# Gate and up product by token instead of by feature, in a one-layer trunk kernel

## The chip, the cores and the metric

The kernel runs on one core of a Trainium2 chip (trn2). The metric is device time in microseconds from launch to end, in several executions; the kernel before has a median of 1082.83 us in 3 runs (1080.88 to 1083.24). PE is the tensor engine, PEld its loading of the operand that stands still, DVE the vector engine, ACT the scalar engine, POOL the GpSimd engine, SP the queue that starts the weight loads.

## The reference

One layer over 256 tokens of width 2048, all in float32. Cut to the part that matters here:

```python
def rmsnorm(x, g):
    return x * lax.rsqrt(jnp.mean(x * x, axis=-1, keepdims=True) + RMS_EPS) * g

x = x + jnp.einsum('bsm,md->bsd', y, w_out)          # y: the two head groups, normalised
h2 = rmsnorm(x, norm2_g)
act = jax.nn.silu(jnp.einsum('bsd,df->bsf', h2, w_gate)) * jnp.einsum('bsd,df->bsf', h2, w_up)
x = x + jnp.einsum('bsf,fd->bsd', act, w_down)       # w_gate, w_up: [2048, 5632]; w_down: [5632, 2048]
```

Ahead of it stands a projection of x to five sections of 1024 columns (v, C, h_B, u, B) with a spatial gating and a short convolution; behind it a last RMSNorm.

## The kernel before

**Precision.** Every matrix operand is cut into a high and a low part of the type float32r (`split`: ACT casts the high part at L82, DVE subtracts it from the source at L83). A product is three products: high by high, low by high, high by low.

**Two forms of product.** The token-major form (`mm_tok`, L121 to L123) holds 128 features of 128 tokens still and moves 512 weight columns, three matmuls of 512 columns. The feature-major form (`mm_feat`, L129 and L130) holds 128 x 128 weights still and moves activations: first the high and the low part of all 256 tokens side by side (512 columns), then with the low weights the high part alone (256 columns). Its result is a PSUM bank of two halves that have to be added (`sum_halves`: ACT copies one half at L152, DVE adds the other at L154).

**Stages.** In order: v (token-major), C with h_B, u, B, w_out (all feature-major, names `ch`, `u`, `b`, `o`), gate and up (feature-major, `gu`), w_down (token-major, `d`). Before the change `gu` runs over 44 tiles f of 128 hidden features, a gate tile and an up tile at once.

**Weights.** They come as units of [128, 2048], each in two halves of 512 KB: one load on SP into `raw` (5 buffers), one cast on ACT to `whi` and one subtraction on DVE to `wlo` (4 buffers each). `next_unit` asks for the next unit when one is taken, so a half is cast into the buffer that the half four places ahead of it has just left. A unit of `gu` feeds 16 matmul pairs.

**Behind each tile f** (`act`, L446 to L453): the two halves are added, the gate is multiplied by 1/rms of its token (`r2b`, a row that every partition holds), ACT takes its sigmoid, DVE multiplies twice, and the result is cut into `aT`, which w_down reads by contraction tile. 1/rms itself needs the sum of squares `sq1`, which POOL gathers behind the last pair of w_out; PE adds it up over the partitions with four small matmuls (`ps_n`, L180), and spreads it over the partitions with one more (`ps_n2b`, L194). The up product keeps its 1/rms open until w_down's result.

**Beside it** `residual` (L456 to L461) turns x to token-major in 8 groups of four 128 x 128 transposes on PE (`ps_x`), for w_down's end.

The order on each engine is made by the tile framework's scheduler from the order of the code and from its own estimates; an engine does its instructions in that order, and waits where an operand or a buffer isn't there.

Of the kernel before, what the change touches and what calls it, by code (L numbers as in the profile page):

```python
# [10 lines left out]
F32 = mybir.dt.float32  # L11
# [5 lines left out]
P = 128  # L17
NW = 512          # one PSUM bank of float32
UN = 2048         # a weight unit is [P, UN], one contiguous load
# [11 lines left out]
def trunk_layer_kernel(  # L31
# [4 lines left out]
    """xt: per-feature vectors as columns, then x by feature, [P, KD, T]; wsj [j, h, i].  # L36

    weights: units of v, (C, h), u, B, out, (gate, up), down in the order of use.
    A token-major product keeps the activations still and moves 512 weight columns;
    a feature-major one keeps 128 weight columns still and moves the high and the low  # L40
    part of all tokens side by side, which leaves the two halves of a bank to be added.
    """
    nc = tc.nc
    T, D = out.shape                  # 256, 2048
    KD = D // P                       # 16
    AW = ln_g.shape[1]                # 1024
    H = wsj.shape[1]                  # 8
    NT = T // P                       # 2 token tiles = gMLP blocks
    KA = AW // P                      # 8
    NC = D // NW                      # 4  # L50
    CA = AW // NW                     # 2
    w_v, w_ch, w_u, w_b, w_o, w_gu, w_d = weights
    NF = w_gu.shape[0] // 2           # 44 tiles of the hidden layer
    KU = UN // NW                     # 4 contraction tiles of a token-major unit

# [34 lines left out]
    def load_unit(piece=HU, between=None):  # L90
        """two halves, each a (hi, lo) pair of [P, HU], loaded and split piece by piece"""
        u = seq.popleft()
        halves = []
        for h in range(2):
            raw, hi, lo = half_tiles()
            for a in range(0, HU, piece):
                s = slice(a, a + piece)
                nc.sync.dma_start(raw[:, s], u[:, h * HU + a:h * HU + a + piece])
                if between is not None:
                    between((h * HU + a) // piece)  # L100
                split(hi[:, s], lo[:, s], raw[:, s])
            halves.append((hi, lo))
        ready.append(halves)

    def next_unit():
        """the next unit, with the one behind it on its way"""
        if seq and len(ready) < 2:
            load_unit()
        return ready.popleft()
# [5 lines left out]
    def mm_tok(acc, at, kk, t, half, j, first, last):  # L115
        """acc += a[tile kk].T @ w, 512 columns"""
        ah = at[:, kk, 0, t * P:(t + 1) * P]
        al = at[:, kk, 1, t * P:(t + 1) * P]
        wh = half[0][:, j * NW:(j + 1) * NW]
        wl = half[1][:, j * NW:(j + 1) * NW]  # L120
        nc.tensor.matmul(acc, lhsT=ah, rhs=wh, start=first, stop=False)  # L121
        nc.tensor.matmul(acc, lhsT=al, rhs=wh, start=False, stop=False)  # L122
        nc.tensor.matmul(acc, lhsT=ah, rhs=wl, start=False, stop=last)  # L123

    def mm_feat(acc, at, kk, half, j, first, last):
        """acc[:, hi | lo] += w.T @ a[tile kk], 128 features by all tokens"""
        wh = half[0][:, j * P:(j + 1) * P]
        wl = half[1][:, j * P:(j + 1) * P]
        nc.tensor.matmul(acc, lhsT=wh, rhs=at[:, kk, :, :], start=first, stop=False)  # L129
        nc.tensor.matmul(acc[:, 0:T], lhsT=wl, rhs=at[:, kk, 0, :], start=False, stop=last)  # L130

    def half_feat(acc, ats, part, unit, first, last, inner=None):
        """contraction tiles part*8..part*8+7 of a pair of feature tiles; inner: work ahead of (j, k)"""
        for j in range(2):
            for k in range(8):
                if inner is not None and (j, k) in inner:
                    inner[j, k]()
                kk = part * 8 + k
                mm_feat(acc[:, j, :], ats[kk // KU], kk % KU, unit[j], k,
                        first and k == 0, last and k == 7)  # L140
# [16 lines left out]
    def split_scaled(dst, k, src, g):  # L157
        """dst hi/lo of tile k = src * g (per partition)."""
# [8 lines left out]
    def rstd_of(ssum, scale, eps, name):  # L167
        """(ssum * scale + eps) ** -0.5 on [P, n]."""
# [7 lines left out]
    def rstd_tokens(sq, scale, eps, name):  # L176
        """sq [P, T]: squares by feature, summed but for the partition -> [token, NT]."""
# [6 lines left out]
    def diagonal(r, name):  # L184
        """[token, NT] -> NT diagonal blocks"""
# [5 lines left out]
    def spread(dg, name, own=False):  # L191
        """the diagonal as the same row of T on every partition"""
# [9 lines left out]
    def add_squares(acc, y, first, name):  # L202
        """acc += the squares of a pair of tiles"""
# [14 lines left out]
    nc.scalar.copy(warm, mhalf[:, 0:1])            # brings in the activation table  # L218
# [5 lines left out]
    NA = 3                                         # pairs of w_out that start with group A alone  # L224
# [3 lines left out]

    xr = [bigtile([P, 2 * KU, T], F32, f"xr{i}") for i in range(KD // (2 * KU))]   # the residual
    xg = units_of(NC, "xg")                        # x * g1, not yet divided by its rms  # L230
    NV = 3 * KD + CONV * KA
    head = const.tile([P, NV + T], F32, name="head")     # the vectors, and the first tile of x
# [13 lines left out]
    # the first unit and the first tiles of x come in single contraction tiles, side by side  # L246
# [12 lines left out]
    # the tensor engine's clock rises while the first loads are under way  # L259
# [11 lines left out]
    def gelu2(acc, t, dst, name):  # L271
        """dst = 2 * gelu(acc * r1), the tanh form."""
# [42 lines left out]
    # spatial weights [j, h, i], chunk-causal: rows of the later chunk feed only its own positions  # L315
# [10 lines left out]
    # LayerNorm of 2v with 4 eps is that of v  # L326
# [15 lines left out]
    def mix(h):  # L342
        """mixed values of heads h, h+1 by feature"""
# [52 lines left out]
    sqB = row("sqB")  # L396
    ra, rb = [], []
    for k in range(0, KA, 2):
        # rms norm of 2y with 4 eps is that of y
# [12 lines left out]
    sq1 = row("sq1")  # L412
    hT = units_of(NC, "hT")                        # x1 * g2, not yet divided by its rms
# [26 lines left out]
    x_tok = const.tile([P, NT, D], F32, name="x_tok")  # L440
    r2 = r2b = None
    aT = units_of(NF // KU, "aT")

    def act(acc, f):
        # silu of the normalised gate times the up product, whose own 1/rms waits for w_down's result
        z = sum_halves(acc, "gu")  # L446
        g, u = z[:, 0, :], z[:, 1, :]
        s = tmp.tile([P, T], F32, tag="b", name="s")
        nc.vector.tensor_tensor(g, g, r2b, op=ALU.mult)
        nc.scalar.activation(s, g, AF.Sigmoid)  # L450
        nc.vector.tensor_tensor(u, u, g, op=ALU.mult)
        nc.vector.tensor_tensor(u, u, s, op=ALU.mult)
        split(aT[f // KU][:, f % KU, 0, :], aT[f // KU][:, f % KU, 1, :], u)  # L453

    def residual(i):
        """the residual by token, for w_down"""  # L456
# [6 lines left out]
    acc0 = gemm_feat(hT, "gu")  # L463
    r2 = rstd_tokens(sq1, 1.0 / D, RMS_EPS, "n2")
    dg2 = diagonal(r2, "n2")
    sp2 = []
    acc1 = gemm_feat(hT, "gu", lambda: sp2.append(spread(dg2, "n2")))
    r2b = sp2[0]
    act(acc0, 0)
    act(acc1, 1)  # L470
    for f in range(2, NF):
        acc = gemm_feat(hT, "gu")
        act(acc, f)
        if f - 2 < NT * NC:
            residual(f - 2)

# [6 lines left out]
    n = NF // KU  # L483

    def x2_of(acc, t, a, w, slot):
        """columns a..a+w of the second residual, and the sum of their squares over D"""
# [9 lines left out]
    for c in range(NC - 1):  # L496
        acc = pacc.tile([P, NT, NW], F32, tag="acc", name=f"d{c}")
        for i in range(n):
            w = next_unit()
            for k in range(KU):  # L500
                for t in range(NT):
                    part(acc[:, t, :], i, w, k, t)
        for t in range(NT):
# [3 lines left out]
    # the last columns: one token tile is finished while the other's last products run  # L507
# [38 lines left out]
def _token_major(w):  # L546
    """[K, N] -> [N/512 * K/512 units, 128, 4 * 512]"""
# [4 lines left out]
def _feature_major(blocks_a, blocks_b):  # L552
    """two [K, n * 128] -> [n pairs * 2 halves of K, 128, (tile of a, tile of b) * 8 * 128]"""
    import numpy as _np

    k, n = blocks_a.shape
    parts = [w.reshape(2, 8, P, n // P, P).transpose(3, 0, 2, 1, 4) for w in (blocks_a, blocks_b)]
# [3 lines left out]
def _pairs(w):  # L561
    """neighbouring tiles of one matrix"""
# [52 lines left out]
```

## Time and profile before

| what | value |
|---|---|
| time, median of 3 runs | 1082.83 us (1080.88 to 1083.24) |
| span of the profiled execution | 1081.1 us (its time with what lies around the span is not given; the median is 1.7 us above the span) |
| PE busy | 1067.5 us, 99% |
| DVE / ACT / POOL busy | 684.2 / 514.3 / 65.4 us |
| stage `gu`, first matmul to the first of `d` | 331.60 to 833.02 us |
| stage `d`, first to last matmul start | 833.02 to 1072.18 us |
| DMA engines busy, whole span | 57.2% for the queue of the weights |

The span is cut into stages by the names of the products: PE goes from one to the next without a pause. A matmul's duration in the rows covers its way through the array, so that several overlap; the time that one costs is the distance from its start to the next one's start.

### The profile page before, as it was taken

What the parts mean: (1) busy time and instruction counts of PE and PEld (TensorE: products, weight loads), DVE (VectorE), ACT (ScalarE), POOL (GpSimd) and SP (SyncE); (2) the same over time, 40 slices, a digit from 0 to 9 for tenths busy, and PEclk for the clock granted to TensorE, in tenths of its full rate; (3) what the DMA queues carried; (4) which work ended last, traced back from release to release, by engine and by line L of the source; (5) the groups of instructions that cost most, each with busy time, mean ns of one, the idle gap of its engine ahead of it and who ended that gap; (6) DMA issues with size and microseconds to landing.
All of it is one profiled execution on the core that took longest, in us unless ns stands there. A gap on an engine that the chain in (4) does not pass through costs nothing.

```text
span 1081.1 us, 14655 instructions
## 1 busy us (share of the span) xinstructions
PE 1067.5 (99%) x5704; PEld 915.1 (85%) x5704; DVE 684.2 (63%) x833; ACT 514.3 (48%) x669; POOL 65.4 (6%) x66
## 2 busy tenths in 40 slices
PE   8999999999999999999999999999999999999996
PEld 7878888888888888888888888888888888888885
DVE  7898667788766666666566665656666445454543
ACT  8453335555554554444444444444444434343432
POOL 4040001232111000000000000000000000000000
PEclk9999999999999999999999999999999999999998
DMA  8846556555555555555555555555556656566652
GB/s 292 258 170 231 176 176 193 183 185 179 195 179 190 178 179 179 186 180 191 185 187 187 183 190 183 190 182 190 184 187 224 200 189 196 192 193 192 194 193 78
DMA packets 58565, 205.33 MB, mean 190 GB/s; under 512 B 6976, under 2 KB 7232, under 8 KB 58368
## 3 DMA queue, kind: packets, MB, share of 16 engines
q1 hardware_dynamic: 57312, 201.39, 57.2%
q10 hardware_dynamic: 1184, 3.02, 0.8%
q8 instruction: 44, 0.72, 0.3%
q14 instruction: 25, 0.20, 0.1%
HBM read 202.28 MB, written 2.10 MB: 189 GB/s over the span
## 4 chain that ended last, share of the span: by engine, by line
PE 94%; issue 3%; DVE 2%; DMA 0%; POOL 0%; ACT 0%; POOLq 0%; DVEq 0%; SPq 0%
PE gu L129 31%; PE gu L130 15%; PE d L123 7%; PE d L122 7%; PE d L121 7%; PE o L129 6%; PE ch L129 4%; PE o L130 3%; PE b L129 3%; PE u L129 3%; PE ch L130 2%; PE b L130 1%; PE u L130 1%; DVE wlo L83 1%; PE v L123 1%
## 5 line engine op out<-in xcount | busy, mean ns | idle before, releaser
L83 DVE TENSOR_TENSOR wlo<-raw,whi 128x1024 fp32r<-128x1024 f32 (+1 forms) x384 | 469.8, 1227 | 336.2 <-ACT whi L82 333.3
L82 ACT CAST whi<-raw 128x1024 fp32r<-128x1024 f32 (+1 forms) x384 | 396.3, 1033 | 482.4 <-issue 142.3
L129 PE MATMUL gu<-hT,whi 128*128 128x512 f32 x1408 | 498.5, 399 | 0.0
L130 PE MATMUL gu<-hT,wlo 128*128 128x256 f32 x1408 | 395.4, 281 | 0.0
L129 PEld LDWEIGHTS gu<-hT,whi 128*128 128x128 f32 x1408 | 264.5, 188 | 65.2
L130 PEld LDWEIGHTS gu<-hT,wlo 128*128 128x128 f32 x1408 | 266.0, 189 | 0.0
L121 PE MATMUL d<-whi,aT 128*128 128x512 f32 x352 | 136.9, 389 | 0.0
L122 PE MATMUL d<-whi,aT 128*128 128x512 f32 x352 | 136.9, 389 | 0.0
L123 PE MATMUL d<-wlo,aT 128*128 128x512 f32 x352 | 136.9, 389 | 0.0
L129 PE MATMUL o<-yT,whi 128*128 128x512 f32 x256 | 90.9, 400 | 0.0
L129 PE MATMUL ch<-xg,whi 128*128 128x512 f32 x256 | 90.5, 398 | 0.0
L122 PEld LDWEIGHTS d<-whi,aT 128*128 128x128 f32 x352 | 66.1, 188 | 13.8
L121 PEld LDWEIGHTS d<-whi,aT 128*128 128x128 f32 x352 | 66.1, 188 | 13.7
L123 PEld LDWEIGHTS d<-wlo,aT 128*128 128x128 f32 x352 | 66.1, 188 | 13.6
L130 PE MATMUL ch<-xg,wlo 128*128 128x256 f32 x256 | 71.9, 281 | 1.9 <-DVE wlo L83 1.9
L130 PE MATMUL o<-yT,wlo 128*128 128x256 f32 x256 | 71.9, 281 | 0.0
L129 PEld LDWEIGHTS o<-yT,whi 128*128 128x128 f32 x256 | 48.1, 188 | 12.0
L129 PEld LDWEIGHTS ch<-xg,whi 128*128 128x128 f32 x256 | 48.1, 188 | 11.5
L130 PEld LDWEIGHTS ch<-xg,wlo 128*128 128x128 f32 x256 | 48.3, 189 | 2.3 <-DVE wlo L83 2.2
L130 PEld LDWEIGHTS o<-yT,wlo 128*128 128x128 f32 x256 | 48.4, 189 | 0.0
L533 POOL TENSOR_TENSOR rf<-sf,mhalf 128x1 f32<-128x1 f32 x2 | 1.1, 552 | 729.5 <-DVE sf L531 729.5
L129 PE MATMUL b<-xg,whi 128*128 128x512 f32 x128 | 45.0, 396 | 0.0
(143 smaller groups left out, 799.0 us busy)
## 6 DMA issues: line engine op xcount, KB each, us to landing
raw<-in_w_gu SPq DMA_DIRECT2D x176, 512.0 KB, 3.6
raw<-in_w_d SPq DMA_DIRECT2D x88, 512.0 KB, 4.4
raw<-in_w_ch SPq DMA_DIRECT2D x32, 512.0 KB, 4.3
raw<-in_w_o SPq DMA_DIRECT2D x32, 512.0 KB, 4.0
raw<-in_w_u SPq DMA_DIRECT2D x16, 512.0 KB, 4.1
raw<-in_w_b SPq DMA_DIRECT2D x16, 512.0 KB, 4.3
raw<-in_w_v SPq DMA_DIRECT2D x16, 256.0 KB, 6.3
raw<-in_w_v SPq DMA_DIRECT2D x8, 512.0 KB, 5.1
```

The lines of the kernel that those rows point to most:

```text
L82: nc.scalar.copy(dst_hi, src)
L83: nc.vector.tensor_tensor(dst_lo, src, dst_hi.bitcast(F32), op=ALU.subtract)
L121: nc.tensor.matmul(acc, lhsT=ah, rhs=wh, start=first, stop=False)
L122: nc.tensor.matmul(acc, lhsT=al, rhs=wh, start=False, stop=False)
L123: nc.tensor.matmul(acc, lhsT=ah, rhs=wl, start=False, stop=last)
L129: nc.tensor.matmul(acc, lhsT=wh, rhs=at[:, kk, :, :], start=first, stop=False)
L130: nc.tensor.matmul(acc[:, 0:T], lhsT=wl, rhs=at[:, kk, 0, :], start=False, stop=last)
L533: nc.gpsimd.tensor_tensor(rf, sf, mhalf[:, 0:1], op=ALU.pow)
```

## The change

The gate and up product becomes token-major. A group g of 256 hidden features (22 groups) has a PSUM tile of two banks, one for each 128 tokens, with 256 gate and 256 up columns side by side. Four weight units make a group, and PE does 96 matmuls of 512 columns in it. The weights are laid out anew on the host for that (`_feature_major` with n > k). Behind a group (`gated`) ACT takes the sigmoid straight from PSUM with 1/rms as its scale by token, and DVE makes two products for each 128 tokens, the second with the up columns from PSUM. The result `a` lies by token; `turned` transposes it on PE with four 128 x 128 transposes into `ps_a`, behind the second unit of the next group, and cuts it into `aT`. The last group is turned in w_down's first columns. The spread of 1/rms (`ps_n2b`, its diagonal and its row) falls away, `residual` stands behind the third unit of each of the first 8 groups, and the four small matmuls `ps_n` behind the first unit of all.

```diff
-    acc0 = gemm_feat(hT, "gu")
-    r2 = rstd_tokens(sq1, 1.0 / D, RMS_EPS, "n2")
-    dg2 = diagonal(r2, "n2")
-    sp2 = []
-    acc1 = gemm_feat(hT, "gu", lambda: sp2.append(spread(dg2, "n2")))
-    r2b = sp2[0]
-    act(acc0, 0)
-    act(acc1, 1)
-    for f in range(2, NF):
-        acc = gemm_feat(hT, "gu")
-        act(acc, f)
-        if f - 2 < NT * NC:
-            residual(f - 2)
+    def gated(acc):
+        a = pair(F32, "z", "a_gu", bufs=2)
+        s = pair(F32, "b", "s_gu")
+        for t in range(NT):
+            nc.scalar.activation(s[:, t, :], acc[:, t, 0:T], AF.Sigmoid, scale=r2[:, t:t + 1])
+        for t in range(NT):
+            nc.vector.scalar_tensor_tensor(s[:, t, :], acc[:, t, 0:T], r2[:, t:t + 1], s[:, t, :],
+                                           op0=ALU.mult, op1=ALU.mult)
+            nc.vector.tensor_tensor(a[:, t, :], s[:, t, :], acc[:, t, T:], op=ALU.mult)
+        return a
+
+    def turned(a, g):
+        ps = pmisc.tile([P, 2, T], F32, tag="pm", name="ps_a")
+        for j in range(2):
+            for t in range(NT):
+                nc.tensor.transpose(out=ps[:, j, t * P:(t + 1) * P], in_=a[:, t, j * P:(j + 1) * P],
+                                    identity=ident)
+        f = 2 * g
+        dst = aT[f // KU]
+        split(dst[:, f % KU:f % KU + 2, 0, :], dst[:, f % KU:f % KU + 2, 1, :], ps)
+
+    for g in range(NG):
+        acc = pacc.tile([P, NT, NW], F32, tag="acc", name="gu")
+        for u in range(NC):
+            w = next_unit()
+            for k in range(KU):
+                for t in range(NT):
+                    mm_tok(acc[:, t, :], hT[u], k, t, w[k // 2], k % 2,
+                           u == 0 and k == 0, u == NC - 1 and k == KU - 1)
+            if g == 0 and u == 0:
+                r2 = rstd_tokens(sq1, 1.0 / D, RMS_EPS, "n2")
+            elif u == 1 and last is not None:
+                turned(*last)
+            elif u == 2 and g < NT * NC:
+                residual(g)
+        last = gated(acc), g
...
+            if i == 1 and held_a:
+                turned(*held_a.pop())
```

What moves on the engines is seen at three places. On PE, at the small matmuls that add up the squares (`ps_n` from `sq`) in the first part of the stage: before, they stand behind all 64 matmuls of the first tile.

```order
L129 MATMUL gu<-hT_2265,whi 128x512
L130 MATMUL gu<-hT_2265,wlo 128x256
L180 MATMUL ps_n_3215<-ones,sq_2261 128x1 [waits Pool_49]
L180 MATMUL ps_n_3215<-ones,sq_2261 128x1
L129 MATMUL gu<-hT_2262,whi 128x512 [waits PE_49]
```

The same matmuls after the change (L183 is L180 of before, L124 to L126 are L121 to L123):

```order
L124 MATMUL gu<-whi,hT_2263 128x512 [waits Activation_49]
L125 MATMUL gu<-whi,hT_2263 128x512
L183 MATMUL ps_n_3163<-ones,sq_2261 128x1 [waits Pool_49]
L183 MATMUL ps_n_3163<-ones,sq_2261 128x1
L126 MATMUL gu<-wlo,hT_2263 128x512 [waits DVE_49]
```

They have moved up: 26 matmuls of the stage stand ahead of them now (the unit's 24, and two that the scheduler put first), and they still wait for POOL's sum.

On PE again, at the transposes: before, only the residual's (`ps_x`) break the row of products.

```order
L129 MATMUL gu<-hT_2265,whi 128x512
L130 MATMUL gu<-hT_2265,wlo 128x256
L460 MATMUL ps_x<-ident,xr_88 128x128 [waits PE_49]
L460 MATMUL ps_x<-ident,xr_88 128x128 x3
L129 MATMUL gu<-hT_2262,whi 128x512 [waits Activation_49]
L130 MATMUL gu<-hT_2262,wlo 128x256 [waits DVE_49]
```

After the change, in the second group, between its second and third unit:

```order
L124 MATMUL gu<-whi,hT_2263 128x512
L125 MATMUL gu<-whi,hT_2263 128x512
L126 MATMUL gu<-wlo,hT_2263 128x512
L471 MATMUL ps_a<-ident,a_gu 128x128 [waits DVE_49,PE_49]
L471 MATMUL ps_a<-ident,a_gu 128x128 [waits DVE_49]
L471 MATMUL ps_a<-ident,a_gu 128x128 x2
L124 MATMUL gu<-whi,hT_2264 128x512 [waits Activation_49]
L125 MATMUL gu<-whi,hT_2264 128x512
```

A second kind of break has come in, four transposes of `a_gu` that wait for DVE, once for each group.

On ACT, for one tile f early in the stage, before:

```order
L152 COPY c_gu<-gu 128x512 [waits PE_49]
L461 COPY x_tok<-ps_x 128x512 [waits PE_49]
L82 CAST whi<-raw 128x1024 [waits DMAHW7_49,PE_49,Activation_49]
L450 ACTIVATE s<-z_gu 128x256 [waits DVE_49]
L82 CAST aT_3115<-z_gu 128x256 [waits DVE_49]
L82 CAST whi<-raw 128x1024 [waits DMAHW0_49,PE_49,Activation_49]
```

And after, one group:

```order
L459 ACTIVATE s_gu<-gu,n_r 128x256 [waits PE_49]
L459 ACTIVATE s_gu<-gu,n_r 128x256
L85 CAST whi<-raw 128x1024 [waits DMAHW7_49,DVE_49,PE_49]
L85 CAST whi<-raw 128x1024 [waits DMAHW0_49,DVE_49,PE_49]
L85 CAST whi<-raw 128x1024 [waits DMAHW1_49,DVE_49,PE_49]
L85 CAST whi<-raw 128x1024 [waits DMAHW2_49,DVE_49,PE_49]
L85 CAST aT_3115<-ps_a 128x2x256 [waits PE_49]
```

The copy of one half has gone; between two groups of sigmoids stand the casts of the weights, and among these the cast of the turned result, behind four of them.

## Rows read from the trace of the kernel before

**Rows 1.** The page, share of the span: busy us, instructions.
```profile
PE 1067.5 (99%) x5704; PEld 915.1 (85%) x5704; DVE 684.2 (63%) x833; ACT 514.3 (48%) x669; POOL 65.4 (6%) x66
```
**Rows 2.** The page, chain of waits that ended last: by engine, by line.
```profile
PE 94%; issue 3%; DVE 2%; DMA 0%; POOL 0%; ACT 0%; POOLq 0%; DVEq 0%; SPq 0%
PE gu L129 31%; PE gu L130 15%; PE d L123 7%; PE d L122 7%; PE d L121 7%; PE o L129 6%; PE ch L129 4%; PE o L130 3%; PE b L129 3%; PE u L129 3%; PE ch L130 2%; PE b L130 1%; PE u L130 1%; DVE wlo L83 1%; PE v L123 1%
```
**Rows 3.** Busy time by stretch: stage gu, then most of d.
```profile
core 0: us, PE busy (x) PEld busy (x) DVE busy (x) ACT busy (x) POOL busy (x), PEclk, DMA share, GB/s
331.60:833.02 501.42, 501.42 (x2857) 435.79 (x2855) 314.03 (x398) 239.87 (x319) 2.29 (x3) 1.00 0.57 186
844.00:1060.00 216.00, 216.00 (x955) 178.91 (x954) 104.54 (x96) 88.34 (x92) 0.00 (x0) 1.00 0.59 188
```
**Rows 4.** Groups by line and shape: count, busy us, mean ns, idle before.
```profile
L129 PE MATMUL gu<-hT,whi 128*128 128x512 f32 x1408 | 498.5, 399 | 0.0
L130 PE MATMUL gu<-hT,wlo 128*128 128x256 f32 x1408 | 395.4, 281 | 0.0
L121 PE MATMUL d<-whi,aT 128*128 128x512 f32 x352 | 136.9, 389 | 0.0
L460 PE MATMUL ps_x<-ident,xr 128*128 128x128 f32 x32 | 4.8, 272 | 0.0
L450 ACT ACTIVATE s<-z_gu 128x256 f32<-128x256 f32 x44 | 18.2, 413 | 0.0
L154 DVE TENSOR_TENSOR z_gu<-gu,c_gu 128x512 f32<-128x512 f32 x44 | 30.1, 684 | 0.0
L488 DVE SCALAR_TENSOR_TENSOR x_tok<-d,n_r,x_tok 128x256 f32<-128x256 f32 x4 | 1.8, 478 | 4.9 <-PE d L123 4.9
```
**Rows 5.** Timeline of PE in gu (start, us, instruction): three pairs apart.
```profile
600.17 0.40 PE L129 MATMUL gu<-hT,whi 128*128 128x512 f32 x1
...
601.23 0.40 PE L129 MATMUL gu<-hT,whi 128*128 128x512 f32 x1
```
**Rows 6.** Timeline of PE in d: its sixth matmul and its last.
```profile
834.18 0.39 PE L123 MATMUL d<-wlo,aT 128*128 128x512 f32 x1
...
1072.18 0.39 PE L123 MATMUL d<-wlo,aT 128*128 128x512 f32 x1
```
**Rows 7.** Timeline of PE in v, around four small matmuls.
```profile
37.13 0.39 PE L123 MATMUL v<-wlo,xg 128*128 128x512 f32 x1
37.36 0.50 PE L180 MATMUL ps_n<-ones,xsq 128*128 128x1 f32 x4
...
38.05 0.40 PE L122 MATMUL v<-whi,xg 128*128 128x512 f32 x1
...
40.13 0.39 PE L122 MATMUL v<-whi,xg 128*128 128x512 f32 x1
```
**Rows 8.** Timeline of PE in gu, around one group of the residual's transposes.
```profile
365.64 0.39 PE L129 MATMUL gu<-hT,whi 128*128 128x512 f32 x1
...
365.99 0.60 PE L460 MATMUL ps_x<-ident,xr 128*128 128x128 f32 x4
...
366.77 0.39 PE L129 MATMUL gu<-hT,whi 128*128 128x512 f32 x1
```
**Rows 9.** Timeline at the start of gu: PE's first matmul, ACT and POOL behind w_out.
```profile
331.60 0.40 PE L129 MATMUL gu<-hT,whi 128*128 128x512 f32 x1
...
334.51 1.05 ACT L82 CAST whi<-raw 128x1024 fp32r<-128x1024 f32 x1 [1.25 <-PE gu L129]
...
337.03 1.67 POOL L210 TENSOR_TENSOR sq<-sq,sq_x 128x256 f32<-128x256 f32 x2 [9.65 <-ACT sq_x L205]
```
**Rows 10.** Timeline of the weights' casts and subtractions late in gu.
```profile
819.01 1.05 ACT L82 CAST whi<-raw 128x1024 fp32r<-128x1024 f32 x1 [1.62 <-issue]
820.10 1.23 DVE L83 TENSOR_TENSOR wlo<-raw,whi 128x1024 fp32r<-128x1024 f32 x1 [1.45 <-ACT whi L82]
821.84 1.05 ACT L82 CAST whi<-raw 128x1024 fp32r<-128x1024 f32 x1 [1.77 <-PE gu L129]
```

More of the change, by code (lines that the diff above doesn't have):

```diff
@@ L52, in trunk_layer_kernel @@
     w_v, w_ch, w_u, w_b, w_o, w_gu, w_d = weights
-    NF = w_gu.shape[0] // 2
+    NG = w_gu.shape[0] // 4
+    NF = 2 * NG
     KU = UN // NW
@@ L440, in trunk_layer_kernel @@
     x_tok = const.tile([P, NT, D], F32, name="x_tok")
-    r2 = r2b = None
     aT = units_of(NF // KU, "aT")
[L444 to L453, printed above, removed]
     def residual(i):
@@ L461, in residual @@
         nc.scalar.copy(x_tok[:, t, c * NW:(c + 1) * NW], ps.rearrange("p k f -> p (k f)"))
-    acc0 = gemm_feat(hT, "gu")
-    r2 = rstd_tokens(sq1, 1.0 / D, RMS_EPS, "n2")
-    dg2 = diagonal(r2, "n2")
-    sp2 = []
-    acc1 = gemm_feat(hT, "gu", lambda: sp2.append(spread(dg2, "n2")))
-    r2b = sp2[0]
-    act(acc0, 0)
-    act(acc1, 1)
-    for f in range(2, NF):
-        acc = gemm_feat(hT, "gu")
-        act(acc, f)
-        if f - 2 < NT * NC:
-            residual(f - 2)
+    def gated(acc):
[17 more added lines that the diff above has]
+        split(dst[:, f % KU:f % KU + 2, 0, :], dst[:, f % KU:f % KU + 2, 1, :], ps)
+    r2 = None
+    last = None
+    for g in range(NG):
[13 more added lines that the diff above has]
+        last = gated(acc), g
     gf = bigtile([P, D], F32, "gf")
@@ L483, in trunk_layer_kernel @@
     n = NF // KU
+    held_a = [last]
     def x2_of(acc, t, a, w, slot):
@@ L556, in _feature_major @@
     k, n = blocks_a.shape
+    if n > k:
+        h = NW // 2
+        both = _np.stack([blocks_a.reshape(k, n // h, h), blocks_b.reshape(k, n // h, h)], axis=2)
+        return _token_major(both.reshape(k, 2 * n))
     parts = [w.reshape(2, 8, P, n // P, P).transpose(3, 0, 2, 1, 4) for w in (blocks_a, blocks_b)]
```

## The prediction, made before the changed kernel ran

> **What bounds the kernel now.** I read the page's busy shares first: PE is busy 99% of the span [rows 1], and the chain of waits gives PE 94%, with the gate and up product (gu) at 31% and 15%, far ahead of the rest [rows 2]. That does not say yet that PE works at its best pace, because overlapping matmuls count as busy. So the second thing I read is distance, not duration. In the stage gu PE is busy for all of its 501.42 us, DVE for 314, ACT for 240, the DMA engines for 0.57 of it, and the granted clock is 1.00, the 2.4 GHz level [rows 3]; neither kind of gu matmul has any idle time ahead of it [rows 4]. The stage costs what PE's row of matmuls costs, one start after the other. The reader is to see that nothing is late in gu: an edit there counts only if it changes how many starts there are, how far apart they stand, or what breaks their row.
>
> **The pace of each form.** In gu three pairs (512 and 256 columns) take 601.23 - 600.17 = 1.06 us, so a pair costs 0.3533 us [rows 5]; 1408 pairs [rows 4] make 497.5 us. The 3.9 us left of 501.42 are the 8 groups of the residual's transposes and the two small jobs for 1/rms. The token-major form is in the trace too, in d: from its sixth matmul to its last, its 1056th (three lines of 352 [rows 4]), 1050 distances take 1072.18 - 834.18 = 238.00 us, so one costs 0.2267 us [rows 6]. It holds that pace with DMA at 0.59, about as much as in gu [rows 3].
>
> **The change, part by part.**
>
> *The products.* 2816 matmuls go, 2112 of 512 columns come (22 groups x 16 contraction tiles x 2 token tiles x 3). At the pace of d they take 2112 x 0.2267 = 478.7 us, against 497.5: 18.8 us less. Both forms move the same number of columns, 1408 x 768 = 2112 x 512; what is saved is what each matmul costs beyond its columns, and there are a quarter fewer of them.
>
> The page "TensorE: Matmul & The Clock Gate" of the Trainium skill, section Back-to-back issue gap, speaks against this: it puts the warm distance at N/2.4 + 2.5 ns, so that a matmul costs next to nothing beyond its columns. By it, as an estimate, the old products would take 457.6 us, the new ones 455.8 us, and 88 transposes would add 4.9 us: about 3 us slower in all. The rows do not agree: they show 353.3 ns for a pair where it has 325, and 226.7 ns where it has 215.8 [rows 5, 6], and it is the difference of these two excesses that I count on.
>
> *The new transposes.* 22 groups of four break the row of products, 21 in gu and one in d. The nearest row by kind is the residual's group, of the same form: from 365.64 to 366.77 lie two pairs and four transposes, 1.13 - 0.707 = 0.42 us for the break [rows 8]. The nearest row by surroundings is the four small matmuls in v, which is token-major: from 37.13 to 40.13 are 11 distances, 3.00 - 11 x 0.2267 = 0.51 us [rows 7]; the excess sits not only in the break, the matmuls behind it stand a few ns too far apart for a while. I take 0.50 for any break of a token-major row, with 0.42 as the lower end. The far upper end is that transposes do not overlap, four times their mean duration of 272 ns [rows 4], or 1.09 us. The same price goes to the 8 residual groups, which stay, and to ps_n.
>
> The same page's section Part 4: PE-mode transpose has about 275 ns for a transpose in a kernel. Our rows have that as a duration, 272 ns, and yet four of them and their aftermath delay the row by 0.42 us [rows 4, 8]. Taken as a cost it gives the rival on transposes below.
>
> *A new wait at the start of gu.* ps_n moves up from behind 64 matmuls to behind 26. It needs POOL's last sum, which ends at 337.03 + 1.67 = 338.70 us [rows 9]. That chain starts behind w_out's last pair and passes, on ACT, behind a cast that waits for PE to leave the first half of gu [rows 9]; this half now takes 12 x 0.2267 = 2.72 us instead of 8 x 0.3533 = 2.83, so the sum comes 0.1 us sooner, at 338.6. PE reaches ps_n at 331.60 + 26 x 0.2267 = 337.5. It waits 1.1 us, and all products queue behind it. Before, the same matmuls were reached after 11.3 us, when the sum was long there. Ends: 0, if the chain on ACT finds a gap, and 2.1, if another cast (1.05 us [rows 9]) slips in front.
>
> *What goes from the other engines.* The copy, addition and row multiplications behind each of 44 tiles go. Per group come two sigmoids on ACT (0.413 each) and a cast, on DVE four operations (0.478 each, from the PSUM operation of d) and one of 512 elements (0.684) [rows 4]; about 2.6 us of DVE in a group of 21.8 us. All of it, gone or new, lies beside PE: I count 0. Spread and diagonal of 1/rms (ps_n2b) take one break out of PE's row; it is inside the 3.9 us above, so its absence needs no term.
>
> *Covers.* Transposes wait for DVE's product: last cast 1.05, two sigmoids 0.83, four DVE operations 1.9, 3.8 us behind the group's end; PE comes there after 48 matmuls, 10.9 us. Weights: a half is cast and subtracted within 821.33 - 819.01 = 2.3 us of its buffer's release [rows 10], and used three halves later, 3 x 2.72 = 8.2 us; 5.9 us are spare, and the sigmoids and DVE operations queued ahead take 2.7 of it. SP's loads keep their order and number. If this cover were gone, each group would pay what is late.
>
> *The sum.* Stage gu: 478.7 + 30 breaks x 0.50 (21 new, 8 residual, ps_n) 15.0 + wait 1.1 = 494.8 us, against 501.42: 6.6 less. Stage d: one break more, 0.5. In all 6.1 us less. Against the profiled execution that is a span of 1081.1 - 6.1 = 1075.0 us; the median of the runs is 1.7 us above the span shown, and I leave that margin as it is: 1082.8 - 6.1 = 1076.7 us.
>
> **The rivals.**
>
> *The row doesn't settle (slower).* Behind a break in v the distances stay wider for nine matmuls: from 38.05 to 40.13, 2.08 us / 9 = 231.1 ns instead of 226.7 [rows 7]. If a row broken every 48 or 96 matmuls stayed there, it would cost 2112 x 4.4 ns = 9.3 us more: 1086.0. At gu's own price per column, 353.3/768 x 512 = 235.5 ns, it would be 18.6 more: 1095.3. It decides from 6.1/2112 = 2.9 ns, a pace of 229.6. For it: gu and d differ though the clock is the same. Against it: d keeps 0.2267 over 1050 matmuls, and v is back at it at 40.13. Chance 5%.
>
> *Transposes at their duration (slower).* 22 x (1.09 - 0.50) = 13.0 us more: 1089.7. Against it stands the residual's group [rows 8]. Chance 3%.
>
> *Weights or gated values late (slower).* If PE stood at each group for what DVE does in a row, 1.9 us, 22 x 1.9 = 42 us more: 1118; it decides from 6.1/22 = 0.28 us a group. For it: one more thing that ACT and DVE do between casts, in order. Against it: the covers of 5.9 and 7.1 us. Chance 3%.
>
> *The gain is eaten (no change).* Breaks at 0.66 instead of 0.50 (31 x 0.16 = 5.0) bring 1081.7. For it: in v the aftermath is seen only behind other matmuls than transposes. Chance 7%.
>
> *Cheaper than I think.* Breaks at 0.42 and no wait: 31 x 0.08 + 1.1 = 3.6 less, 1073.1; inside the forecast's range, with 3% below it.
>
> **How the numbers follow.** My forecast, 1073 to 1080.6, has 79%; with the 3% below it, faster by over 0.2% (2.2 us, about what a measurement of this kernel tells from no change) has 82%. Within 0.2%, 1080.7 to 1085.0, are the 7% of the eaten gain and 1% of the first rival's lower part. Slower: the rest of the three rivals, 10%. The range, 1073.0 to 1081.5, leaves out the slower rivals and part of the eaten gain.
>
> **What would show it.** Right: gu's rows have starts 0.2267 apart, the groups with transposes are 0.4 to 0.5 us longer than 96 x 0.2267 = 21.8 us, the waits have one line of PE's ps_n on POOL of about 1 us and no other of gu, and the stage has 494 to 496 us. Wrong: starts 0.230 or more apart between breaks; idle time ahead of ps_a or of the first matmul of a unit; more than 0.6 us for a break.

## The result, and the profile after

The changed kernel takes 1076.27 us (median of 5 runs, 1075.33 to 1078.57), the kernel before, run beside it, 1083.24 (median of 5). The ratio is 0.9935, 95% interval 0.9919 to 0.9951: 7.0 us less, where 6.1 were forecast. The profiled execution of after took 1075.33 us with a span of 1073.5. Here and below an execution that took twice as long as the others (one of the kernel before, one of experiment 7) is left out.

The page after: busy shares, then the chain of waits by engine and by line.

```profile
PE 1059.6 (99%) x5086; PEld 887.2 (83%) x5086; DVE 634.3 (59%) x721; ACT 492.6 (46%) x602; POOL 66.7 (6%) x66
...
PE 93%; issue 3%; DVE 2%; DMA 1%; ACT 0%; POOL 0%; SPq 0%; POOLq 0%; DVEq 0%
PE gu L126 15%; PE gu L124 15%; PE gu L125 15%; PE d L125 7%; PE d L126 7%; PE d L124 7%; PE o L132 6%; PE ch L132 4%; PE o L133 3%; PE b L132 3%; PE u L132 3%; PE ch L133 2%; PE b L133 1%; PE u L133 1%; DVE wlo L86 1%
```

PE has 99% as before [rows 1]. DVE lost 50 us of work and ACT 22, and the shares of the chain hardly move: gu now has 45% where it had 46% [rows 2]. What the change is worth stands in the stages. Busy time by stretch in after (columns as in [rows 3]): stage gu, then most of d.

```profile
331.09:825.24 494.15, 493.24 (x2235) 408.54 (x2233) 263.58 (x286) 218.05 (x253) 3.15 (x3) 1.00 0.57 190
840.00:1055.00 215.00, 215.00 (x950) 178.19 (x949) 104.50 (x95) 87.42 (x92) 0.00 (x0) 1.00 0.56 186
```

Stage gu has 494.15 us instead of 501.42 [rows 3]: 7.3 less, at the same granted clock of 1.00 and the same DMA share. PE is idle in it for 0.91 us, and the timeline of after (start, us, instruction, idle before and what ended it) shows where, how a group with transposes looks, and where d begins and ends:

```profile
331.09 0.40 PE L124 MATMUL gu<-whi,hT 128*128 128x512 f32 x1
...
336.82 0.39 PE L125 MATMUL gu<-whi,hT 128*128 128x512 f32 x1
338.12 0.61 PE L183 MATMUL ps_n<-ones,sq 128*128 128x1 f32 x4 [0.91 <-POOL sq L213]
338.59 0.48 PE L126 MATMUL gu<-wlo,hT 128*128 128x512 f32 x1
...
546.86 0.39 PE L126 MATMUL gu<-wlo,hT 128*128 128x512 f32 x1
547.09 0.60 PE L471 MATMUL ps_a<-ident,a_gu 128*128 128x128 f32 x4
547.44 0.48 PE L124 MATMUL gu<-whi,hT 128*128 128x512 f32 x1
...
569.32 0.60 PE L471 MATMUL ps_a<-ident,a_gu 128*128 128x128 f32 x4
...
825.24 0.39 PE L124 MATMUL d<-whi,aT 128*128 128x512 f32 x1
...
1064.84 0.39 PE L126 MATMUL d<-wlo,aT 128*128 128x512 f32 x1
```

From one ps_a to the next are 22.23 us; 96 products at 0.2267 make 21.76, so the break costs 0.47. At ps_n the products on either side stand 338.59 - 336.82 = 1.77 us apart, at a ps_a 547.44 - 546.86 = 0.58. Stage d takes 239.60 us from its first matmul to its last, against 239.16 before (833.02 to 1072.18). The rest of the span's 7.6 us lies outside these two stages: gu began 0.5 us earlier, in a part that the change does not touch (v's first matmul started at 4.85 us instead of 5.75, and v lost some of that again), and 0.2 us lie behind d.

The groups of after (line, tiles, shape and count, busy us and mean ns, idle before):

```profile
L124 PE MATMUL gu<-whi,hT 128*128 128x512 f32 x704 | 276.9, 393 | 0.0
L471 PE MATMUL ps_a<-ident,a_gu 128*128 128x128 f32 x88 | 13.1, 272 | 0.0
L461 DVE SCALAR_TENSOR_TENSOR s_gu<-gu,n_r,s_gu 128x256 f32<-128x256 f32 x44 | 21.1, 479 | 1.0 <-ACT s_gu L459 1.0
L86 DVE TENSOR_TENSOR aT<-ps_a,aT 128x512 fp32r<-128x512 f32 x22 | 15.1, 686 | 0.0
```

Neither the products nor the transposes have idle time ahead of them: the gated values are never late.

### The profile page after: what moved, and what is told of

It reads as the page before. It is cut to its first block, busy times and chain, and to the rows that moved or that the text cites. A ratio compares the mean times of both kernels' runs of the same rounds, so it can differ in the third digit from the quotient of the medians.

```text
span 1073.5 us, 13218 instructions
## 1 busy us (share of the span) xinstructions
PE 1059.6 (99%) x5086; PEld 887.2 (83%) x5086; DVE 634.3 (59%) x721; ACT 492.6 (46%) x602; POOL 66.7 (6%) x66
## 4 chain that ended last, share of the span: by engine, by line
PE 93%; issue 3%; DVE 2%; DMA 1%; ACT 0%; POOL 0%; SPq 0%; POOLq 0%; DVEq 0%
PE gu L126 15%; PE gu L124 15%; PE gu L125 15%; PE d L125 7%; PE d L126 7%; PE d L124 7%; PE o L132 6%; PE ch L132 4%; PE o L133 3%; PE b L132 3%; PE u L132 3%; PE ch L133 2%; PE b L133 1%; PE u L133 1%; DVE wlo L86 1%
## 5 line engine op out<-in xcount | busy, mean ns | idle before, releaser
L124 PE MATMUL gu<-whi,hT 128*128 128x512 f32 x704 | 276.9, 393 | 0.0
L126 PE MATMUL gu<-wlo,hT 128*128 128x512 f32 x704 | 274.8, 390 | 0.0
L125 PE MATMUL gu<-whi,hT 128*128 128x512 f32 x704 | 274.5, 390 | 0.0
L126 PEld LDWEIGHTS gu<-wlo,hT 128*128 128x128 f32 x704 | 132.2, 188 | 27.6
L125 PEld LDWEIGHTS gu<-whi,hT 128*128 128x128 f32 x704 | 132.4, 188 | 26.6
L124 PEld LDWEIGHTS gu<-whi,hT 128*128 128x128 f32 x704 | 132.3, 188 | 26.5
L124 PE MATMUL d<-whi,aT 128*128 128x512 f32 x352 | 137.2, 390 | 0.0
L126 PE MATMUL d<-wlo,aT 128*128 128x512 f32 x352 | 137.1, 390 | 0.0
L124 PEld LDWEIGHTS d<-whi,aT 128*128 128x128 f32 x352 | 66.1, 188 | 13.8
L126 PEld LDWEIGHTS d<-wlo,aT 128*128 128x128 f32 x352 | 66.1, 188 | 13.5
L132 PEld LDWEIGHTS ch<-xg,whi 128*128 128x128 f32 x256 | 48.1, 188 | 11.5
```

## The experiments

**Theories.** All start from the result that the row of PE's starts is the time. The question is why the new row is shorter, and what its breaks cost. Theory: fewer, longer matmuls save what each costs beyond its columns. Rival: the old row of 512 and 256 in turn stood at a bad pace for a reason of its own, which could be had without the change. The breaks (the places where other work interrupts the row of products) are settled first.

**1. Turning left out.**

```diff
-        ps = pmisc.tile([P, 2, T], F32, tag="pm", name="ps_a")
-                nc.tensor.transpose(out=ps[:, j, t * P:(t + 1) * P], in_=a[:, t, j * P:(j + 1) * P], identity=ident)
-        split(..., ps)
+        split(..., a)
```

> The changed kernel without the 22 groups of transposes: the gated result is cut into aT as it lies, by token, so the turning is left out and w_down multiplies other numbers. If a break costs what the distances of the changed kernel show, 22.233 - 96 x 0.2267 = 0.47 us a group, stage gu falls from 494.1 to 484.2 us and the whole by 22 x 0.47 = 10.4 us, to about 1066 us. If the transposes stood in time that PE would have lost anyway (to ACT's or DVE's order at the group's end), the stage keeps more than 490 us. If they cost their duration of 0.272 each, it falls by 24 us.

First matmul of gu and of d in this kernel:

```profile
331.86 0.40 PE L124 MATMUL gu<-whi,hT 128*128 128x512 f32 x1
...
816.08 0.39 PE L124 MATMUL d<-whi,aT 128*128 128x512 f32 x1
```

The stage has 484.22 us, 9.93 less than in after: 0.473 for each of 21 breaks. The whole has 1065.01 us, ratio 0.9829 (0.9811 to 0.9847).

**2. Turning done twice.**

```diff
-        for j in range(2):
+        for j in (0, 1, 0, 1):
```

> The changed kernel with each group's four transposes done twice into the same PSUM, 88 transposes more and no break more. If four transposes cost their distances, 4 x 0.1085 = 0.43 us, stage gu grows by 21 x 0.43 = 9.1 us to 503.3 us, and the settling behind the break (some 0.04 us of 0.47) is paid once. If the price of a break sat in the change of form and not in the transposes, it grows by less than 3 us. At their duration it would grow by 23 us.

```profile
331.46 0.40 PE L124 MATMUL gu<-whi,hT 128*128 128x512 f32 x1
...
834.81 0.39 PE L124 MATMUL d<-whi,aT 128*128 128x512 f32 x1
```

These are the same two starts: 503.35 us, 9.20 more for 21 times four transposes, 0.44 a group or 110 ns for one, though each lasts 272 ns. Transposes behind one another overlap as other matmuls do; the break is nearly all their own distances.

**3. 1/rms two units later.** `rstd_tokens` moves from behind the first unit of group 0 to behind the third, ahead of `residual(0)`.

```diff
-            if g == 0 and u == 0:
-                r2 = rstd_tokens(sq1, 1.0 / D, RMS_EPS, "n2")
             elif u == 2 and g < NT * NC:
+                if g == 0:
+                    r2 = rstd_tokens(sq1, 1.0 / D, RMS_EPS, "n2")
                 residual(g)
```

> The changed kernel with the four small matmuls of 1/rms moved from behind the first unit to behind the third, right ahead of the first residual's transposes. If the wait on POOL's sum costs what the trace shows (1.77 us from the last matmul ahead of the break to the next behind it, against 0.58 for other breaks), PE loses 1.2 us less, and one break less has to settle (0.05 us): stage gu 492.9 us instead of 494.1. If that wait was cover for weights that are late, another wait takes its place in the first group and the stage stays at 494. A measurement of the whole time can hardly tell 1.2 us; the trace can.

The timeline of this kernel where PE reaches ps_n:

```profile
347.44 0.39 PE L126 MATMUL gu<-wlo,hT 128*128 128x512 f32 x1
347.67 0.50 PE L183 MATMUL ps_n<-ones,sq 128*128 128x1 f32 x4
348.03 0.64 PE L451 MATMUL ps_x<-ident,xr 128*128 128x128 f32 x4
348.42 0.48 PE L124 MATMUL gu<-whi,hT 128*128 128x512 f32 x1
```

No idle time stands there now, and the stage has 492.92 us, 1.2 less: the wait was real and avoidable. The whole has 1075.07 us, ratio 0.9927 (0.9913 to 0.9942), which overlaps the interval of after; only the stage shows the gain.

**4. More work on DVE.** In `gated`, four more operations a group:

```diff
+        for _ in range(2):
+            for t in range(NT):
+                nc.vector.tensor_tensor(more[:, t, :], s[:, t, :], acc[:, t, T:], op=ALU.mult)
```

> The changed kernel with four more operations on DVE behind each group, products of the gated values into a tile that nobody reads: 22 x 4 x 0.42 us = 37 us more of DVE, queued ahead of the weights' subtractions. The prediction counted everything on DVE and ACT behind a group at nothing, with 5.9 us to spare for the weights. If that holds, stage gu stays at 494.1 to 494.4 us and PE has no new idle time. If DVE's order sets when weights are there, up to 1.7 us a group come on the path, 37 us in all.

The waits of PE in this kernel (us in total, times, longest), the one that lies in gu:

```profile
PE ps_n L183 <- POOL sq L213: 0.9, 1, 0.9
```

The added tile had 88 operations of 411 ns, 36 us in all. The stage has 494.16 us, as after; the whole, in a single run, 1077.39. More work on DVE in gu costs nothing. That the work which the change took away gained nothing either is not tested by a run; it follows from the rows of before, where no gu matmul has idle time ahead of it [rows 4].

**5. Small breaks in the old form.** Behind every tile of before that has no residual group: one to three small matmuls (c; the trace has two instructions for each) or one to four transposes (t), in turn.

```diff
             residual(f - 2)
+        else:
+            probe(*KINDS[f % len(KINDS)])      # c1 c2 c3 t1 t2 t3 t4
```

> The kernel before, with one extra break in PE's row behind each of the tiles f = 10 to 43, in seven kinds by turns: one, two or three one-column matmuls of ones (c1, c2, c3), or one to four 128 x 128 transposes of the identity (t1 to t4), into PSUM that nobody reads. Theory A (one pace): a feature-major pair costs 353.3 ns whatever stands ahead of it; each break then only adds 0.1 to 0.45 us, and stage gu grows by 34 x some 0.27 = 9 us, to 510 us. Theory B (two paces): the pair has a fast pace of about 346.7 ns, seen in the kernel before in stage u and between ps_n and ps_x, and a slow one of 353.3 ns, and a break decides which of the two follows. Then some kinds of break are followed by 32 pairs at 346.7 ns, 0.21 us less for each such tile, and the stage grows by less than 9 us; if all kinds did it, by about 2 us.

The stage has 509.62 us (whole 1091.61, one run). That is near the 510 that one theory expected, but the rows show that it came out so by chance, for the pairs behind the breaks stand at two paces. The timeline around a break by one transpose:

```profile
458.66 0.40 PE L129 MATMUL gu<-hT,whi 128*128 128x512 f32 x1
...
459.72 0.40 PE L129 MATMUL gu<-hT,whi 128*128 128x512 f32 x1
...
460.07 0.27 PE L471 MATMUL ps_t1x<-ident 128*128 128x128 f32 x1
...
460.53 0.40 PE L129 MATMUL gu<-hT,whi 128*128 128x512 f32 x1
...
462.61 0.40 PE L129 MATMUL gu<-hT,whi 128*128 128x512 f32 x1
```

Ahead of it three pairs take 1.06 us, 353.3 ns each; behind it six take 2.08, 346.7 each. In this kernel t1, t3 and c2 left the row of gu at 346.7 ns each time, and t2, t4, c1 and c3 at 353.3. That does not show that the kind of break decides: t1, t3 and c2 always came upon the slower pace, t2, t4 and c3 always upon the faster one, and of the eight residual groups, four transposes each, one was followed by the faster pace and seven by the slower. The kernel before has both paces as well. In gu, between ps_n2b and the first residual group:

```profile
354.89 0.39 PE L129 MATMUL gu<-hT,whi 128*128 128x512 f32 x1
...
356.97 0.39 PE L129 MATMUL gu<-hT,whi 128*128 128x512 f32 x1
```

Six pairs take 2.08 us here. In its first tile, and from the first residual group (366 us) to the end of gu, it stands at 353.3 ns, in 1344 of the 1408 pairs: 1344 x 6.67 ns = 9.0 us that are no price of a matmul.

**6. One tick to put it right.** The lever that this suggested: one transpose of the identity (a `tick`) in before, behind tile 10, or five transposes in place of four in all eight residual groups:

```diff
             residual(f - 2)
+        elif f == 10:                 # the second kernel: a tick() behind each residual(f - 2)
+            tick()
```

> The kernel before with a single 128 x 128 transpose of the identity (0.1 us) put into PE's row behind tile f = 10, and nothing else. In the run with seven kinds of break, one transpose was followed by the fast pace of 346.7 ns a pair each time, where it came on a slow row. Theory A (a feature-major pair costs 353.3 ns): stage gu stays at 501.4 to 501.6 us and the whole at 1083 us. Theory B (two paces, and half of the change's saving on the products is the slow pace): 33 tiles of 32 pairs go on at 346.7 ns, 33 x 32 x 6.6 ns = 7.0 us less, stage gu 494.5 us and the whole about 1076 us, the changed kernel's time without its change; if the row slips back to the slow pace on the way, something between.

> The kernel before with a fifth transpose (of the identity) in each of the residual's 8 breaks. Theory A: 8 x 0.11 = 0.9 us more, stage gu 502.3 us. Theory B: if five transposes lead to the fast pace from either pace, all tiles but the first stand at 346.7: 8 x 32 x 6.6 ns = 1.7 and 34 x 32 x 6.6 ns = 7.2 less, stage gu 493.4 us. If the pace that follows depends on the pace ahead too, fast and slow tiles take turns, and the long rest behind the last break is all fast (494.5) or all slow (501.5).

The first kernel, its tick and the row late in gu:

```profile
461.14 0.27 PE L465 MATMUL ps_tick<-ident 128*128 128x128 f32 x1
...
462.65 0.40 PE L129 MATMUL gu<-hT,whi 128*128 128x512 f32 x1
...
464.77 0.40 PE L129 MATMUL gu<-hT,whi 128*128 128x512 f32 x1
...
599.75 0.40 PE L129 MATMUL gu<-hT,whi 128*128 128x512 f32 x1
...
601.87 0.40 PE L129 MATMUL gu<-hT,whi 128*128 128x512 f32 x1
```

Right behind the tick and late in gu six pairs take 2.12 us, 353.3 ns each: the row stayed at the slower pace. The stage has 501.41 us, the ratio is 1.0001 (0.999 to 1.0013). With five transposes one of eight breaks was followed by the faster pace, and the stage has 501.96, ratio 1.0009 (0.9996 to 1.0022). The lever fails: one transpose behind tile 10 led to the faster pace in experiment 5 and not here.

The order of the instructions alone does not set the pace either. Ahead of gu the first kernel gives PE the same 1794 matmuls and transposes as before, in the same order. Yet in stage `u` six pairs take 2.08 us in before:

```profile
169.83 0.39 PE L129 MATMUL u<-xg,whi 128*128 128x512 f32 x1
...
171.91 0.39 PE L129 MATMUL u<-xg,whi 128*128 128x512 f32 x1
```

and 2.12 us in this kernel:

```profile
169.81 0.40 PE L129 MATMUL u<-xg,whi 128*128 128x512 f32 x1
...
171.93 0.40 PE L129 MATMUL u<-xg,whi 128*128 128x512 f32 x1
```

In the long part of `o` it is the other way round, 353.3 ns a pair in before and 346.7 here. What sets the pace stays open.

**7. Ticks in the earlier stages.** On experiment 3, single ticks in `ch`, in the mixing behind it and in `o`.

```diff
         acc = gemm_feat(xg, "ch")
+        if k == 0:
+            tick()
...
             mix(2 * (k - (KA - H // 2)))
+            if k == KA - 2:
+                tick()
...
         half_feat(accs[i], yT, 1, next_unit(), False, True)
+        if i == 0:
+            tick()
```

> The changed kernel with the late small matmuls of the fourth run, and one transpose of the identity at three places of the feature-major stages that stand at the slow pace: behind the first tile of C and h_B, behind the third of its mixing products, and in w_out. Stage gu as in the fourth run, 492.9 us. Theory B: some 150 + 30 + 210 pairs go from 353.3 to 346.7 ns, 2.6 us less, for 3 x 0.13 us: the whole 2.2 us below the fourth run, about 1072.8 us. Theory A: 0.4 us above it.

1075.70 us (median of five), ratio 0.9922 (0.9905 to 0.994): no better than experiment 3. The tick in `ch` led from the slower to the faster pace, but only up to a wait of PE for DVE 11 us later, behind which the row stood at the slower one again; the tick in the mixing came upon the faster pace, which went on; the one in `o` led from the faster to the slower. And `ch` was 1.4 us longer for another reason (last section).

**8. The new form with the lengths of the old.** Here activations stand still and weights move, as in after, but the third matmul is cut into two of 256. In the first kernel both follow one another (512, 512, 256, 256), in the second they alternate with the long ones:

```diff
-                    mm_tok(...)                     # ah wh, al wh, ah wl: 512, 512, 512
+    first kernel:   ah wh (512), al wh (512), ah wl[:256], ah wl[256:]
+    second kernel:  ah wh (512), ah wl[:256], al wh (512), ah wl[256:]
```

> The changed kernel with the last of each three matmuls of stage gu cut into two of 256 columns, 512, 512, 256, 256: 2816 matmuls, as many as the feature-major form has, for the same columns, still by token. Theory C (each matmul costs 13.3 ns beyond its columns, which is what 226.7 ns for 512 columns at 2.4 GHz, and the fast pair of 346.7 ns for 768, both give): 704 x 13.3 ns = 9.4 us more, stage gu 503.5 us, which is above the feature-major stage of 501.4 because the 21 new breaks and the wait stay. If the excess belongs to the form and not to the count, the stage stays at 494 to 496 us. If mixed lengths bring the slow pace (6.6 ns more for 768 columns), up to 9.3 us come on top, 512.8 us.

> As the run before it, but in the order 512, 256, 512, 256, the lengths of the feature-major row. Theory C with the slow pace as a thing of alternating lengths: 503.5 us at the fast pace, 512.8 us at the slow one, and with a break each 48 to 96 matmuls both may be seen, one behind some breaks and the other behind others. If the slow pace belongs to the feature-major operands (a large moving tile of activations) and not to the lengths, 503.5 us throughout, as in the run before.

The timeline of the first, nine rounds of 1536 columns:

```profile
603.35 0.40 PE L133 MATMUL gu<-whi,hT 128*128 128x512 f32 x1
...
609.62 0.40 PE L133 MATMUL gu<-whi,hT 128*128 128x512 f32 x1
```

and of the second, nine pairs:

```profile
603.21 0.40 PE L135 MATMUL gu<-whi,hT 128*128 128x512 f32 x1
...
606.39 0.40 PE L133 MATMUL gu<-whi,hT 128*128 128x512 f32 x1
```

The first has 6.27 / 18 = 348.3 ns for 768 columns, near the faster pace, and a stage of 505.55 us (whole 1086.12): 11.4 more than after, for 704 more matmuls 16.2 ns each, somewhat more than the 13.3 expected. The second has 3.18 / 9 = 353.3 ns, the old form's slower pace to the digit, and a stage of 511.15 (whole 1094.43; one run each). Both paces occur in it: five stretches between breaks, about a tenth of its matmuls, stand at 346.7. So 17.0 of the 18.8 us that the products save come back when only the lengths and their order are the old ones. At equal lengths and order, which operand stands still is worth next to nothing.

**9. The old form with its lengths grouped.** Before and experiment 3, where `half_feat` does eight matmuls of 512 and then the eight of 256, with the same operands:

```diff
-                mm_feat(acc[:, j, :], ats[kk // KU], kk % KU, unit[j], k, ...)
+                nc.tensor.matmul(acc[:, j, :], lhsT=unit[j][0][...], rhs=ats[kk // KU][:, kk % KU, :, :], ...)
+            for k in range(8):
+                nc.tensor.matmul(acc[:, j, 0:T], lhsT=unit[j][1][...], rhs=ats[kk // KU][:, kk % KU, 0, :], ...)
```

> The kernel before, all products still feature-major, with the order of the matmuls changed in the feature-major stages: for each feature tile first the eight of 512 columns, then the eight of 256, instead of 512 and 256 by turns. Count, columns and operands are the same. If the slow pace comes from the alternation of lengths, the row goes at 13.3 ns beyond the columns: stage gu 1408 x 346.7 ns + 3.9 = 492 us, 9.3 us less, and some 3.3 us in the other feature-major stages, the whole about 1071 us, below the changed kernel. If the pace does not hang on the order, 501.4 us and no change; if short matmuls in a row cost more than their columns and 13.3 ns (as the loads of the standing operand, 188 ns each, may make them), more than before.

> The changed kernel with the late small matmuls of the fourth run and the grouped order of the run before in the stages that stay feature-major (C with h_B, u, B, w_out). If the alternation of lengths brings the slow pace, some 500 of these 768 pairs gain 6.6 ns, 3.3 us: stage gu 492.9 us as in the fourth run, the whole about 1071.8 us. If not, the fourth run's time, 1075 us.

The timeline of before so edited: gu's first matmul, eight pairs late in gu, the first of d:

```profile
328.81 0.40 PE L139 MATMUL gu<-hT,whi 128*128 128x512 f32 x1
...
601.37 2.00 PE L139 MATMUL gu<-hT,whi 128*128 128x512 f32 x8
603.21 1.11 PE L143 MATMUL gu<-hT,wlo 128*128 128x256 f32 x8
604.17 0.40 PE L139 MATMUL gu<-hT,whi 128*128 128x512 f32 x1
...
824.84 0.40 PE L121 MATMUL d<-whi,aT 128*128 128x512 f32 x1
```

Eight pairs take 2.80 us here; over the whole stretch behind the last residual group (444.86 to 824.72 us) it is 349.2 ns a pair, between the two paces. A group of eight pairs thus costs some 20 ns more than at the faster pace, which I had not counted (492 was expected). The stage has 496.03 us, 5.4 less than before, and the whole 1074.75, ratio 0.9913 (0.99 to 0.9927), since the four feature-major stages ahead of gu got the same edit. `ch` alone went from 95.67 to 92.99 us; part of that is PE's wait for DVE's `wlo` there, 1.9 us in before and gone here, where the low part is needed later. As a whole this edit without the change gains about as much as the change or more (the intervals overlap); in gu alone it gains less, 5.4 us against 7.3. With both, and 1/rms late, the kernel takes 1071.43 us, ratio 0.9882 (0.9868 to 0.9895). That is the best version; the change and experiment 3 together make 3.3 us of its gain over the grouped kernel.

## Why the prediction was right, and which reason was not

- *Bound.* Right: what counts is the distance of PE's starts. PE has no idle time in the stage but the wait at ps_n, and 36 us more on DVE had no effect on it (experiment 4).
- *Pace of the new row, 226.7 ns.* Right between the breaks, from the first group to the last, once the few matmuls behind a break have settled. The rival of a row that does not settle, 229.6 or more, is out.
- *Why it is shorter.* The step "what is saved is what each matmul costs beyond its columns, and there are a quarter fewer of them" holds for one half only. At one column a cycle (a pair takes 640 ns at 1.2 GHz, last section) 768 columns are 320 ns at 2.4 GHz; the faster pace of 346.7 ns leaves 13.3 for each matmul, as 226.7 does for 512 columns. So 704 fewer matmuls are 704 x 13.3 ns = 9.4 us; the other 9.0 are the slower pace at which the alternating row stood (experiments 5 and 8). I read 353.3 from three pairs and took it as the price of the form for all 1408. But 64 of them stood at 346.7, so that the 497.5 us were 0.4 too high and the 3.9 us left 0.4 too low; and of what the others cost beyond their columns a fifth, 6.67 of 33.3 ns, was the slower pace and no price of the form. The number does not rest on this reason, because both paces were read from rows. But it holds only where the old row stands at its slower pace, as it does in the long stretch of gu in all three profiles that have it (before and both kernels of experiment 6). At the faster pace the advice would be the other one: as an estimate from these numbers, 9.4 us do not pay for the new breaks and the wait, 22 x 0.47 + 1.2 = 11.5 us.
- *Breaks at 0.50.* Measured 0.47 with all that follows them. The Trainium skill, "TensorE: Matmul & The Clock Gate", Part 4: PE-mode transpose, has about 275 ns for one; the traces agree as to the duration, 272, and not as a cost, 110.
- *The wait at ps_n, 1.1 us.* Measured 1.77 - 0.58 = 1.2, of which 0.91 show as idle. Moving ps_n gave 1.2 back (experiment 3). POOL's sum came 0.5 us earlier than I had worked out, and so did PE.
- *Covers.* Right: no wait of PE in gu but that one.
- *The same page's Back-to-back issue gap*, N/2.4 + 2.5 ns for the isolated gap of a warm matmul, by which the change would have been 3 us slower, is not borne out: no settled row here stands below 226.7 ns at 512 columns (it has 215.8), and eight matmuls of 256 take 0.96 us in experiment 9, 120 each (it has 109.2).
- *Stage d*, 0.5 forecast, 0.44 measured. The whole, 6.1 forecast, 7.0 measured: of the difference 0.65 lies in gu (494.8 and 494.15), mainly 30 breaks at 0.47 instead of 0.50.

## What to carry to other kernels

Where PE is busy all the time, measure the distance between starts, split it into columns and rest, and ask whether the rest is the form's or the order's: one kernel with the same lengths in another order tells. In this case matmuls of two lengths in turn stood at either of two paces, and not always at the same one in the same program. A row of one length stood at one pace throughout, and lengths in groups of eight came to 349.2 ns a pair, which needs no transposes. Four transposes in this busy row cost about two products (0.47 us), and a small matmul that waits for a slow engine belongs where its operand is already there.

## What was not expected of the hardware

The two paces of 512 and 256 in turn, 346.7 and 353.3 ns at the same granted clock of 1.00; that the pace may be another one behind a break; and that the same instructions stood at the one in one execution and at the other in another (experiment 6). The cause stays open.

In some executions a pause of some 2 us cost more than itself. In experiment 7, in `ch`, PE waits for DVE; windows and the matmuls behind:

```profile
77.00:80.00 3.00, 0.96 (x7) 0.56 (x5) 3.00 (x2) 1.53 (x2) 1.84 (x1) 1.00 0.00 0
80.00:84.00 4.00, 4.00 (x14) 3.46 (x15) 3.85 (x7) 0.00 (x0) 0.00 (x0) 0.58 0.50 157
```

```profile
79.99 0.39 PE L133 MATMUL ch<-xg,wlo 128*128 128x256 f32 x1 [2.04 <-DVE wlo L86]
...
81.11 0.63 PE L132 MATMUL ch<-xg,whi 128*128 128x512 f32 x1
81.75 0.63 PE L132 MATMUL ch<-xg,whi 128*128 128x512 f32 x1
```

Behind 2.04 us without work the granted clock is 0.58 from 80 to 84 us, and a pair takes 640 ns, its columns at the lower level of 1.2 GHz. In the kernel before, the same stretch behind a wait of 1.91 us kept the upper level:

```profile
80.00:84.00 4.00, 4.00 (x24) 3.46 (x23) 3.96 (x6) 1.05 (x1) 0.00 (x0) 1.00 0.68 204
```

Experiment 6's first kernel and both of experiment 8 show the drop too, behind waits of 1.9 us as in before. `ch` is 1.4 to 1.5 us longer where it shows (1.0 in the first of 8, whose row went on at the faster pace). That may be part of the spread between executions: of 22 of the kernel before beside experiment 6, the eight with a mean granted clock of 0.996 or less took 1085.0 us on average, the other 14 took 1083.1. The runs don't show why one execution falls and another does not.
